# Moving the sums and low parts of shared operands, v's weight sums and the key/value low parts from a choice of two engines to VectorE alone

## The chip, the core and the metric

The kernel runs on one core of one Trainium2 chip. A core has five engines with an instruction queue each: TensorE (PE) multiplies matrices into PSUM, VectorE (DVE) and GpSimd (POOL) do elementwise work, ScalarE (ACT) copies and applies functions, SyncE (SP) here issues the DMAs. Each engine works through its queue in order, and semaphores hold an instruction until its inputs are there. The metric is the device time of one execution in microseconds (us).

## The reference, cut to what matters

One decoder block over 1024 tokens of width 1024, all in float32:

```python
h = x
h = h + hybrid_mixer(rmsnorm(h, norm_mix), w_in, ...)            # Mamba-2 branch and gated linear attention branch
h = h + mem_cross_attention(rmsnorm(h, norm_xattn), rmsnorm(mem, norm_mem), w_xq, w_xkv, w_xo)
h = h + swiglu(rmsnorm(h, norm_ffn), w_ffn_in, w_ffn_out)        # width 2816
return rmsnorm(h, norm_final)
```

`hybrid_mixer` begins with one wide product, `n @ w_in`, whose columns are split into z, xBC, dt, q, k, v, r, a1 and two gates. The cross-attention's keys and values are `m @ w_xkv` of 256 memory tokens. Nearly all the arithmetic is in such products.

## The kernel before

**Products in parts.** TensorE takes float32 operands rounded to a shorter form (`F32R`). To keep float32 accuracy each operand x is split into a high part, `hi = round(x)`, and a low part, `lo = x - hi`, and a product is the sum of three: hi·hi, hi·lo, lo·hi. The helper `split` (line 223) does it: ScalarE writes `hi`, and a subtraction writes `lo`, on the engine given by its argument `e`, or on VectorE if none is given.

**Seven products for eight.** A big product is a two-by-two block product done with seven multiplications (B11, B21, T1, B22, T2, T3, T4; a Strassen-Winograd scheme). For that, sums and differences of blocks are formed on both sides. The side that is shared by many units (the normalised activations) is prepared once by the class `Operands` (lines 231 to 274): for each of the seven names and each k it may first combine two blocks in place (`comb`, line 272; in T1, T2, T3 and T4) and then split the block (line 273) into tiles such as `B11h` and `B11l`. For x the blocks are in tiles `hs`, for the feed-forward part in tiles `o`. `upto` hands the steps out one by one between products. The side of one unit (a stripe of 256 weight columns) is prepared in `Unit.left` (line 295), with sums in tiles `sa` and `raw`.

**The first stages.** `kv_unit` (line 550) computes keys and values of the memory tokens from `w_xkv`: it splits the weights, two blocks of 128 rows at a time, into `whi` and `wlo` (line 563). `x_steps` (line 586) works out the norm of x (`xr`, spread over the partitions by way of `diag` tiles and TensorE) and transposes x into `hs`. `v_steps` (line 637) computes v with the scheme in which the weights are the moving side: it loads the weights into `vraw`, forms their sums in `vsa` and in place (lines 652 to 662), and splits them. A loop at line 699 and the call at line 710 interleave these three. After them come the other column groups of `w_in` with the two recurrences between them (up to about 900 us), five dense products, the attention, and from about 1340 us the feed-forward part, whose shared operands are built while the dense product before it runs (line 1471).

**Who does what.** `either` (line 85) picks VectorE or GpSimd for one instruction while the program is written. It keeps a ledger for each engine (class `Meter`): a guess when the engine will be done, set forward by each instruction that it gets, and by TensorE's own estimated time. GpSimd is taken if it would end earlier by this ledger, with `slack` us in its favour:

```python
def either(ap, slack=0.0):
    return POOL if POOL.after(ap) - slack < DVE.after(ap) else DVE
```

`either` is used at other places too (`Unit.left`, statistics, gates of the feed-forward part). The order of the instructions in each engine's queue is written by the tile framework: it plans all instructions by priority against a simulated clock (`schedule_with_timeline_sim=True`, line 1675); work inside `with ahead():` is given a priority 200 steps earlier. The lines that the program names for elementwise work on both engines are all line 73, the ledger's wrapper; so groups are told apart by their tiles.

Of the kernel before, what the change touches and what calls it, by code (L numbers as in the profile page):

```python
# [78 lines left out]
def block_kernel(ctx: ExitStack, tc: tile.TileContext, t: dict, out: bass.AP):  # L79
# [3 lines left out]
    DVE, POOL = Meter(nc.vector, now, 0.06, 1.04e-3), Meter(nc.gpsimd, now, 0.08, 2.25e-3)  # L83

    def either(ap, slack=0.0):

        return POOL if POOL.after(ap) - slack < DVE.after(ap) else DVE
# [34 lines left out]
    def acc():  # L122
        return ps.tile([P, 512], F32, name="acc", tag="acc", bufs=4)
# [4 lines left out]
    add = lambda e, o, a, b: e.tensor_tensor(o, a, b, ALU.add)  # L128
    sub = lambda e, o, a, b: e.tensor_tensor(o, a, b, ALU.subtract)
# [12 lines left out]
    def slot(key, shape=(P, 2, TOK), dt=F32, name="sl"):  # L142
        pl, n = slots[key]
        return pl.tile(list(shape), dt, name=name, tag="sl", bufs=n)
# [78 lines left out]
    def split(src, hi, lo, e=None):  # L223
        ACT.activation(hi, src, AF.Copy)  # L224
        sub(e or DVE, lo, src, hi)

    def wring():

        return [wp.tile([P, 640], F32R, name=n, tag=n, bufs=3)[:, :528] for n in ("whi", "wlo")]

    class Operands:
# [30 lines left out]
        def build(s, hb, kh, first):  # L262
            blk = hb if callable(hb) else lambda: hb
            for name in s.order:
                new, of, comb = s.PLAN[name]
                o = s.B[name] = [slot(s.last_key if name == "T4" else s.key, (P, kh, HALF), F32R, name=name + x) for x in "hl"]
                for k in range(kh):
                    q = lambda ij: blk()[ij[0] * kh + k][:, half(ij[1] ^ s.swap)]
                    for ij in new:
                        first(ij[0] * kh + k, ij[1] ^ s.swap, q(ij))  # L270
                    if comb:
                        comb[0](either(q(of), 1.0), q(of), q(comb[1]), q(comb[2]))
                    split(q(of), o[0][:, k], o[1][:, k], either(q(of)))
                    yield

    class Unit:
# [37 lines left out]
        def q(s, i, j):  # L314
            return s.o[:, i, half(j)]
# [195 lines left out]
    def load_kv_w(c0):  # L511
        kv_raw[c0] = slot("op", (P, NB, 256), name="raw")
        SP.dma_start(kv_raw[c0], t["w_xkv"][:, c0:c0 + 256].rearrange("(k p) c -> p k c", p=P))
# [36 lines left out]
    def kv_unit(c0):  # L550

        n = kv_cols.index(c0)
        for c in kv_cols[n:n + 4]:
            if c not in kv_raw:
                load_kv_w(c)
        raw = kv_raw[c0]
        pa = [kv_bank[0](), kv_bank[0]()]
        for kk in range(4):
            with ahead():
                hi, lo = wring()  # L560
                hv = hi[:, :512].rearrange("p (k c) -> p k c", c=256)
                lv = lo[:, :512].rearrange("p (k c) -> p k c", c=256)
                split(raw[:, 2 * kk:2 * kk + 2, :], hv, lv, either(lo))
            for i in range(2):
                o = pa[i][:, :256]
                for k2 in range(2):
                    k = 2 * kk + k2
                    for m, (x, y) in enumerate(((hv, mh), (lv, mh), (hv, ml))):
                        w_, m_ = x[:, k2, :], y[:, k, :]
                        if c0 < D:  # L570
                            PE.matmul(o, w_[:, i * P:(i + 1) * P], m_, start=k == 0 and m == 0, stop=k == 7 and m == 2)
                        else:
                            PE.matmul(o, m_[:, i * P:(i + 1) * P], w_, start=k == 0 and m == 0, stop=k == 7 and m == 2)
            yield
        s = stg.tile([P, 2, 256], F32, name="kvs", tag="st")
        for i in range(2):
            if c0 < D:
                mul(DVE, s[:, i], pa[i][:, :256], mbc)
            else:
                ACT.activation(s[:, i], pa[i][:, :256], AF.Copy, scale=mss[:, i:i + 1])  # L580
        if c0 < D:
            SP.dma_start(kT_d[c0:c0 + 256, :].rearrange("(i p) m -> p i m", p=P), s)
        else:
            SP.dma_start(vm_d[:, c0 - D:c0 - D + 256].rearrange("(i p) c -> p i c", p=P), s)
# [40 lines left out]
    def load_v(pr):  # L625
        if pr not in vraw:
            rr = vraw[pr] = [vp.tile([P, 4, 2 * HW], F32, name="vraw", tag=f"vraw{h}") for h in range(2)]
            for i in range(2):
                v0 = V0 + 512 * pr + 256 * i
                a0 = (DT0, A0)[pr] + 8 * i  # L630
                for h in range(2):
                    for c0, n, o in ((v0, 256, i * HW), (a0, 8, i * HW + 256)):
                        SP.dma_start(rr[h][:, :, o:o + n],
                                     w_in[512 * h:512 * h + 512, c0:c0 + n].rearrange("(k p) c -> p k c", p=P))
        return vraw[pr]

    def v_steps():
        for pr in range(2):
            rr = load_v(pr)
            A11, A21 = rr[0][:, :, :HW], rr[0][:, :, HW:]  # L640
            A12, A22 = rr[1][:, :, :HW], rr[1][:, :, HW:]
            s = {ij: vp.tile([P, 4, HW], F32, name="vq", tag=f"vq{ij[0]}{ij[1]}") for ij in
                 ((0, 0), (0, 1), (1, 0), (1, 1))}
            small = (dt_t, a1_t)[pr]

            def vfin(i, j, ap):
                SP.dma_start(v_d[half(j), 512 * pr + 256 * i:512 * pr + 256 * i + 256]
                             .rearrange("(a p) c -> p a c", p=P), ap[:, :, :256])
                POOL.tensor_copy(small[:, 4 * j:4 * j + 4, 8 * i:8 * i + 8], ap[:, :, 256:])

            sa = vp.tile([P, 4, HW], F32, name="vsa", tag="vsa")
            for n, name in enumerate(CHAIN):
                parts = []
                with ahead():
                    e = either(A11, 2.0)
                    if name == "T1":
                        add(e, sa, A21, A22)
                    elif name == "B22":
                        sub(e, sa, sa, A11)
                        sub(either(A11, 2.0), A12, A12, sa)  # L660
                    elif name == "T3":
                        sub(e, A21, A11, A21)
                    a = (A11, A12, sa, A12, sa, A21, A22)[n]
                    for k2 in range(2):
                        hi, lo = wring()
                        hv, lv = hi.rearrange("p (k c) -> p k c", c=HW), lo.rearrange("p (k c) -> p k c", c=HW)
                        split(a[:, 2 * k2:2 * k2 + 2, :], hv, lv)
                        parts.append((hv, lv))
                xh, xl = B[name]
                if n in (0, 2, 4):  # L670
                    pa = [acc()[:, :HW] for _ in range(4)]
                for a4 in range(4):
                    p = pa[a4]
                    m = 0
                    for k in range(4):
                        wh, wl = (q[:, k % 2, :] for q in parts[k // 2])
                        for x, w in ((xh, wh), (xl, wh), (xh, wl)):
                            PE.matmul(p, x[:, k, a4 * P:(a4 + 1) * P], w, start=n in (0, 2, 4) and m == 0, stop=m == 11,
                                      skip_group_check=True)
                            m += 1  # L680
                    g = lambda i, j: s[i, j][:, a4, :]
                    with ahead():
                        if n == 0:
                            ACT.activation(g(1, 0), p, AF.Copy)
                        elif n == 1:
                            ACT.activation(g(0, 0), p, AF.Copy)
                        else:
                            ij = ((1, 1), (0, 1), (0, 1), (1, 1), (1, 0))[n - 2]
                            add(DVE, g(*ij), p, g(*ij) if n > 3 else g(1, 0))
                    B.upto((n + 1) * B.kh + a4 + 1)  # L690
                    yield
                ij = (None, (0, 0), None, None, (0, 1), (1, 1), (1, 0))[n]
                if ij:
                    vfin(*ij, s[ij])

    kvg = chain(kv_unit(c) for c in kv_cols)
    xg = x_steps()
    load_v(0)
# [7 lines left out]
    drain(xg)  # L706
    turn_rest()
    vg = v_steps()
    kv_bank[0] = bank
    run(vg, (kvg, 1.2))  # L710
# [968 lines left out]
```

## Time and profile before

| | |
|---|---|
| median of 3 runs | 1998.22 us (1995.6 to 1999.11) |
| span of the profiled execution | 2000.0 us |
| PE busy | 1933.5 us (97%), 9772 products |
| DVE busy | 1330.8 us (67%), 1869 instructions |
| ACT busy | 866.3 us (43%), 1486 instructions |
| POOL busy | 658.0 us (33%), 482 instructions |
| mean granted TensorE clock | 0.992 |

Everything in the profile is of one execution. A row of a group gives line, engine, operation, `out<-in` by the program's names, shapes and count, then after the bar the busy time and the mean duration in ns, then the idle time of that engine before these instructions and who ended it. A row of a timeline begins with start and length in us; the bracket gives the idle time before it and its releaser. A row of the table by stretch gives start and end, length, and the busy time with the count of PE, PEld (weight loads), DVE, ACT and POOL, then the granted clock, the DMA engines' share and GB/s. A row of waits gives who waited for whom, the total, the number of waits and the longest. Durations of neighbouring instructions overlap by some hundredths of a us, since the end of one runs into the start of the next.

### The profile page before, as it was taken

What the parts mean: (1) busy time and instruction counts of PE and PEld (TensorE: products, weight loads), DVE (VectorE), ACT (ScalarE), POOL (GpSimd) and SP (SyncE); (2) the same over time, 40 slices, a digit from 0 to 9 for tenths busy, and PEclk for the clock granted to TensorE, in tenths of its full rate; (3) what the DMA queues carried; (4) which work ended last, traced back from release to release, by engine and by line L of the source; (5) the groups of instructions that cost most, each with busy time, mean ns of one, the idle gap of its engine ahead of it and who ended that gap; (6) DMA issues with size and microseconds to landing.
All of it is one profiled execution on the core that took longest, in us unless ns stands there. A gap on an engine that the chain in (4) does not pass through costs nothing.

```text
span 2000.0 us, 26313 instructions
## 1 busy us (share of the span) xinstructions
PE 1933.5 (97%) x9772; PEld 1619.0 (81%) x9772; DVE 1330.8 (67%) x1869; ACT 866.3 (43%) x1486; POOL 658.0 (33%) x482
## 2 busy tenths in 40 slices
PE   6899999999999999999999999999999999999998
PEld 6799677787777877888888888877888888878887
DVE  5856579979887566643553427478777777784465
ACT  7434745455553555543223226453333333354243
POOL 3521253445654121112442100155444444430002
PEclk9899999999999999999999999999999999999999
DMA  9332233365663754697674310333224223176463
GB/s 303 137 123 76 97 127 116 107 199 162 181 192 103 213 162 158 226 394 242 252 249 163 106 43 22 126 124 124 79 90 134 93 85 119 72 269 220 153 228 126
DMA packets 242019, 309.59 MB, mean 155 GB/s; under 512 B 16586, under 2 KB 164276, under 8 KB 241892
## 3 DMA queue, kind: packets, MB, share of 16 engines
q1 hardware_dynamic: 241892, 307.92, 46.1%
q8 instruction: 77, 1.26, 0.3%
q14 instruction: 50, 0.41, 0.1%
HBM read 211.07 MB, written 96.80 MB: 154 GB/s over the span
## 4 chain that ended last, share of the span: by engine, by line
PE 69%; DVE 12%; DMA 7%; ACT 5%; issue 3%; POOL 3%; SPq 0%; POOLq 0%; DVEq 0%; ACTq 0%
PE acc L51 61%; PE bank L51 7%; DVE wlo L73 3%; DVE cv L73 2%; DVE o L73 1%; PE bank L55 1%; DMA raw<-in_w_in_dram 1%; DMA h_d<-ga 1%; DMA sr<-sr_d 1%; ACT whi L224 1%; DMA csb<-cs_d 1%; POOL sa L73 1%; DMA xt<-in_x_dram 1%; DMA fr<-act_d 1%; DVE fs L73 1%
## 5 line engine op out<-in xcount | busy, mean ns | idle before, releaser
L51 PE MATMUL acc<-hl,wd 128*128 128x512 f32 x1920 | 439.2, 390 | 0.2 <-DVE hl L73 0.2
L51 PEld LDWEIGHTS acc<-hl,wd 128*128 128x128 f32 x1920 | 360.0, 188 | 75.3 <-DVE hl L73 0.6
L73 DVE TENSOR_TENSOR wlo<-raw,whi 128x512 fp32r<-128x512 f32 x264 | 243.1, 925 | 64.9 <-ACT whi L224 64.5
L224 ACT ACTIVATE whi<-raw 128x512 fp32r<-128x512 f32 x272 | 169.7, 628 | 237.0 <-PE acc L51 208.1
L73 DVE TENSOR_TENSOR o<-acc,o 128x512 f32<-128x512 f32 (+1 forms) x256 | 172.5, 675 | 105.8 <-PE acc L51 91.1
L51 PE MATMUL acc<-fs 128*128 128x512 f32 (+1 forms) x792 | 156.0, 356 | 1.8 <-ACT o L1574 1.7
L51 PEld LDWEIGHTS acc<-fs 128*128 128x128 f32 x792 | 130.6, 189 | 22.8 <-ACT o L1574 2.1
L73 POOL TENSOR_TENSOR raw<-raw,sa 128x512 f32<-128x512 f32 x48 | 65.0, 1354 | 253.8 <-DVE wlo L73 250.8
L224 ACT ACTIVATE fs<-fr 128x1024 fp32r<-128x1024 f32 (+1 forms) x84 | 80.1, 984 | 112.9 <-PE acc L51 38.6
L73 DVE TENSOR_TENSOR fs<-fr,fs 128x1024 fp32r<-128x1024 f32 (+1 forms) x84 | 99.8, 1218 | 38.5 <-ACT fs L224 38.0
L224 ACT ACTIVATE whi<-sa 128x512 fp32r<-128x512 f32 x96 | 59.9, 627 | 107.5 <-PE acc L51 107.4
L73 POOL TENSOR_TENSOR sa<-raw 128x512 f32<-128x512 f32 x47 | 75.8, 1613 | 82.0 <-DMA raw<-in_w_in_dram 44.8
L73 DVE TENSOR_TENSOR wlo<-sa,whi 128x512 fp32r<-128x512 f32 x96 | 82.8, 863 | 19.0 <-ACT whi L224 17.6
L224 ACT ACTIVATE wd<-raw 128x1024 fp32r<-128x1024 f32 x40 | 42.2, 1058 | 104.9 <-PE acc L51 104.4
L73 DVE TENSOR_TENSOR wd<-raw,wd 128x1024 fp32r<-128x1024 f32 x40 | 53.9, 1349 | 50.5 <-ACT wd L224 50.0
L73 POOL TENSOR_TENSOR raw<-raw 128x512 f32<-128x512 f32 x48 | 83.0, 1730 | 5.0 <-DVE sa L73 5.0
L51 PE MATMUL acc<-B21h,whi 128*128 128x512 f32 x192 | 76.3, 398 | 3.1 <-ACT o L353 3.1
L51 PE MATMUL acc<-T1h,whi 128*128 128x512 f32 x192 | 76.3, 397 | 2.8 <-ACT whi L224 2.8
L51 PE MATMUL acc<-B22h,wlo 128*128 128x512 f32 x192 | 77.0, 401 | 1.2 <-DVE wlo L73 1.2
L51 PE MATMUL acc<-B22h,whi 128*128 128x512 f32 x192 | 75.2, 392 | 2.6 <-DVE o L73 1.5
L51 PE MATMUL acc<-T4h,whi 128*128 128x512 f32 x192 | 75.9, 395 | 1.5 <-DVE o L73 1.5
L51 PE MATMUL acc<-T1h,wlo 128*128 128x512 f32 x192 | 76.8, 400 | 0.5 <-DVE wlo L73 0.5
(386 smaller groups left out, 4771.6 us busy)
## 6 DMA issues: line engine op xcount, KB each, us to landing
raw<-in_w_in_dram SPq DMA_DIRECT2D x26, 1024.0 KB, 6.1
raw<-in_w_ffn_in_dram SPq DMA_DIRECT2D x22, 1024.0 KB, 6.3
act_d<-o SPq DMA_DIRECT2D x77, 256.0 KB, 2.1
fr<-act_d SPq DMA_DIRECT2D x35, 512.0 KB, 6.4
pre<-in_w_ffn_out_dram SPq DMA_DIRECT2D x11, 1024.0 KB, 6.1
fr<-down_d SPq DMA_DIRECT2D x20, 512.0 KB, 3.7
down_d<-pre SPq DMA_DIRECT2D x33, 256.0 KB, 5.2
raw<-in_w_xkv_dram SPq DMA_DIRECT2D x8, 1024.0 KB
```

The costliest lines, as they stand in the source:

```text
L51: return s.e.matmul(o, x, y, **kw)
L55: return s.e.transpose(o, x, i)
L73: return f(*a, **kw)
L224: ACT.activation(hi, src, AF.Copy)
```

## The change

At three places the choice between VectorE and GpSimd is taken away and VectorE is named. In `Operands.build` these are the combinations of blocks and the low parts; in `kv_unit` the low parts of the key/value weights; in `v_steps` the sums of v's weights. `split` without its last argument uses VectorE. Nothing else in the program text changes; the ledgers that `either` reads elsewhere are still kept.

```diff
@@ Operands.build
                     if comb:
-                        comb[0](either(q(of), 1.0), q(of), q(comb[1]), q(comb[2]))
-                    split(q(of), o[0][:, k], o[1][:, k], either(q(of)))
+                        comb[0](DVE, q(of), q(comb[1]), q(comb[2]))
+                    split(q(of), o[0][:, k], o[1][:, k])
@@ kv_unit
-                split(raw[:, 2 * kk:2 * kk + 2, :], hv, lv, either(lo))
+                split(raw[:, 2 * kk:2 * kk + 2, :], hv, lv)
@@ v_steps
-                    e = either(A11, 2.0)
                     if name == "T1":
-                        add(e, sa, A21, A22)
+                        add(DVE, sa, A21, A22)
                     elif name == "B22":
-                        sub(e, sa, sa, A11)
-                        sub(either(A11, 2.0), A12, A12, sa)
+                        sub(DVE, sa, sa, A11)
+                        sub(DVE, A12, A12, sa)
                     elif name == "T3":
-                        sub(e, A21, A11, A21)
+                        sub(DVE, A21, A11, A21)
```

## The prediction

> **What bounds the kernel now.** I read the page's engine totals and its chain first.
>
> ```profile
> PE 1933.5 (97%) x9772; PEld 1619.0 (81%) x9772; DVE 1330.8 (67%) x1869; ACT 866.3 (43%) x1486; POOL 658.0 (33%) x482
> PE 69%; DVE 12%; DMA 7%; ACT 5%; issue 3%; POOL 3%; SPq 0%; POOLq 0%; DVEq 0%; ACTq 0%
> ```
>
> TensorE (PE) is busy for 97% of the span, so a change on VectorE (DVE) and GpSimd (POOL) can only matter where PE stands still. The edits touch three places: the preparation of x, mem and v (up to about 180 us) and the operands of the feed-forward part (about 1260 to 1360 us). So the next view is the table of busy time by stretch. Its columns are the stretch, its length, then busy time and count of PE, PEld, DVE, ACT and POOL, the granted clock, and the DMA share and rate.
>
> ```profile
> 22.20:44.60 22.40, 16.35 (x125) 14.98 (x123) 15.14 (x20) 15.28 (x32) 13.82 (x11) 0.91 0.82 249
> 44.60:73.90 29.30, 19.18 (x126) 17.91 (x125) 29.28 (x28) 16.67 (x34) 22.71 (x14) 0.78 0.70 253
> 73.90:118.80 44.90, 44.74 (x368) 44.47 (x369) 32.85 (x52) 19.97 (x37) 7.37 (x5) 1.00 0.15 51
> 130.00:200.00 70.00, 70.00 (x488) 65.69 (x487) 38.14 (x71) 29.68 (x54) 16.29 (x21) 1.00 0.30 96
> 1336.00:1362.00 26.00, 22.10 (x93) 17.38 (x92) 26.00 (x27) 15.02 (x28) 19.15 (x13) 0.93 0.38 127
> ```
>
> In 44.6 to 73.9 us (call it B) DVE works without a pause, 29.28 of 29.30 us, while PE is idle for 10 us and its clock drops to 0.78. The same holds for 1336 to 1362 us (C): DVE 26.00 of 26.00, PE idle 3.9 us. Between them PE is full (44.74 of 44.90, 70.00 of 70.00). The view of waits says what PE waits for:
>
> ```profile
> PE bank L51 <- DVE wlo L73: 6.4, 1, 6.4
> PE bank L51 <- DVE diag L73: 5.0, 2, 4.3
> PE acc L51 <- ACT o L353: 2.3, 1, 2.3
> ```
>
> The first two lie before 75 us, the third in C, where that ACT copy stands behind DVE work. In all three places the bound is DVE's queue, and the change puts more work on it. The question is whether this work costs DVE more or less than what GpSimd's running beside it costs now.
>
> **What moves.** The groups of GpSimd that the three edits name:
>
> ```profile
> L73 POOL TENSOR_TENSOR hs<-hs 128x512 f32<-128x512 f32 x14 | 22.7, 1648 | 7.6 <-DVE B11l L73 6.4 <-DVE T1l L73 1.3
> L73 POOL TENSOR_TENSOR wlo<-raw,whi 128x512 fp32r<-128x512 f32 x8 | 10.7, 1352 | 20.7 <-ACT whi L224 18.5 <-PE bank L55 2.2
> L73 POOL TENSOR_TENSOR vsa<-vraw 128x1056 f32<-128x1056 f32 x2 | 5.4, 2702 | 8.5 <-DMA vraw<-in_w_in_dram 8.5
> L73 POOL TENSOR_TENSOR vraw<-vraw 128x1056 f32<-128x1056 f32 x2 | 5.2, 2600 | 0.1
> L73 POOL TENSOR_TENSOR vsa<-vsa,vraw 128x1056 f32<-128x1056 f32 x2 | 4.9, 2470 | 4.5 <-DVE wlo L73 4.5
> L73 POOL TENSOR_TENSOR B11l<-o,B11h 128x512 fp32r<-128x512 f32 x4 | 5.4, 1343 | 160.1 <-ACT B11h L224 160.1
> L73 POOL TENSOR_TENSOR B22l<-o,B22h 128x512 fp32r<-128x512 f32 x2 | 3.5, 1750 | 0.0
> L73 POOL TENSOR_TENSOR B21l<-o,B21h 128x512 fp32r<-128x512 f32 x1 | 1.3, 1291 | 3.5 <-ACT B21h L224 3.5
> L73 POOL TENSOR_TENSOR o<-o x12: 1285/1396/1799, 1273.7 to 1349.3; 128x512 f32<-128x512 f32 x12
> ```
>
> That is 47 instructions: 14 combinations of x's blocks, 8 low parts of key/value weights, 6 sums of v's weights, and in the feed-forward part 7 low parts and 12 combinations. The low parts of x's operands are on DVE already. No DMA and no TensorE work moves.
>
> What does one cost on DVE? Look at a moment when GpSimd rests, and at an operation that reads only one operand from SBUF (the other comes from PSUM):
>
> ```profile
> 75.76 1.89 DVE L73 TENSOR_TENSOR B22l<-hs,B22h 128x512 fp32r<-128x512 f32 x3
> 75.00:80.00 5.00, 5.00 (x44) 5.00 (x43) 3.67 (x7) 2.25 (x6) 0.00 (x0) 1.00 0.20 67
> L73 DVE SCALAR_TENSOR_TENSOR hs<-bank,cols,rbc 128x512 f32<-128x512 f32 x8 | 5.7, 742 | 1.8 <-ACT rbc L598 1.8
> L73 DVE TENSOR_TENSOR B21l<-hs,B21h 128x512 fp32r<-128x512 f32 x4 | 6.2, 1586 | 0.0
> L73 DVE COPY cols<-bank 128x90 f32<-128x90 f32 x1 | 0.2, 240 | 0.0
> ```
>
> With GpSimd silent, three 128x512 operations take 1.89 us, 0.63 us each. The same shape takes 1586 ns (B21l) in B, where GpSimd is busy 22.71 us; the last three rows are DVE's groups in B. The eight operations from PSUM take 742 ns in that same stretch. So it isn't a slow DVE: operations with two SBUF operands, and only these, are held while GpSimd runs. GpSimd's share of the work is paid for on DVE.
>
> **A, 22.2 to 44.6 us.**
>
> ```profile
> 22.32 1.28 POOL L73 TENSOR_TENSOR wlo<-raw,whi 128x512 fp32r<-128x512 f32 x1 [14.08 <-ACT whi L224]
> 24.76 0.48 DVE L73 TENSOR_SCALAR diag<-ident,xr 128x128 f32<-128x128 f32 x2 [1.13 <-POOL xr L73]
> 27.22 1.11 DVE L73 TENSOR_SCALAR diag<-ident,xr 128x128 f32<-128x128 f32 x1 [1.25 <-PE bank L51]
> 33.46 1.50 DVE L73 TENSOR_SCALAR diag<-ident,xr 128x128 f32<-128x128 f32 x2
> 37.48 2.84 DVE L73 TENSOR_TENSOR wlo<-vraw,whi 128x528 fp32r<-128x528 f32 x1
> 40.24 2.62 DVE L73 TENSOR_SCALAR diag<-ident,xr 128x128 f32<-128x128 f32 x2
> 37.32 2.44 POOL L73 TENSOR_TENSOR vsa<-vraw 128x1056 f32<-128x1056 f32 x1 [2.64 <-DMA vraw<-in_w_in_dram]
> 39.83 2.75 POOL L73 TENSOR_TENSOR vraw<-vraw 128x1056 f32<-128x1056 f32 x1
> L73 DVE TENSOR_TENSOR vraw<-vraw,vsa 128x1056 f32<-128x1056 f32 x2 | 2.5, 1252 | 2.6 <-POOL vsa L73 2.6
> ```
>
> Time freed on the chain: the first low part, 1.28 to 0.63, 0.65; the diag at 27.22, 1.11 against 0.24 (half of the pair of 0.48), 0.87; the pair at 33.46, 1.50 against 0.48, 1.02; the wlo at 37.48, 2.84 against about 0.65 (528 columns), 2.19; the pair at 40.24, which ends as the 1056-column operation does, 2.62 against 0.48, 2.14. Sum 6.9. Added to DVE: five low parts at 0.63 and two sums of v's weights at 1.25, 5.65. All of it on the path leaves 1.2; all hidden in DVE's 7.3 idle us (22.40 less 15.14) leaves 6.9. I take 3, nearer the lower end, since the two sums can't start before their load lands at 37.3 and the last idle gap before 44.6 is short. Queued behind them are the diag pair, PE's 4.3 us wait, and everything of B.
>
> **B, 44.6 to 73.9 us.** Of its 28 DVE instructions eight come from PSUM and one is the small copy; the other 19 have two SBUF operands. Unheld: 19 x 0.63 + 8 x 0.70 + 0.24 = 17.8 us. The four combinations of T1 must come before the T1 low parts: 4 x 0.63, 20.3. The ten others (T2 to T4) may fall here, 6.3 more, 26.6, or later. So the stretch shortens by 2.7 to 9.0 us. I take 6, about half of the ten inside. PE, busy 19.18 us at a lowered clock, isn't the floor.
>
> What carries the gain on: behind 73.9 PE is full. There the left-over combinations, three low parts and one 1.25 us sum lie on DVE's 12 idle us (44.90 less 32.85), at price 0; if that cover is gone, each costs PE 0.63. The second half of v (sums at 1.25 each) lies under PE's 70.00 of 70.00, DVE 38.14: 0.
>
> **C, 1336 to 1362 us, and before it.**
>
> ```profile
> L73 DVE TENSOR_TENSOR T2l<-o,T2h 128x512 fp32r<-128x512 f32 x4 | 4.8, 1228 | 0.0
> L73 POOL TENSOR_TENSOR o<-o 128x512 f32<-128x512 f32 x3 | 4.9, 1646 | 2.6 <-ACT o L1469 2.6
> L73 POOL TENSOR_TENSOR raw<-raw,sa 128x512 f32<-128x512 f32 x2 | 3.5, 1751 | 3.0 <-DVE rstd L73 3.0
> L73 POOL TENSOR_TENSOR raw<-raw 128x512 f32<-128x512 f32 x2 | 3.0, 1512 | 0.0
> L73 POOL TENSOR_TENSOR sa<-raw 128x512 f32<-128x512 f32 x2 | 2.8, 1390 | 1.2 <-DVE wlo L73 1.2
> 1310.00:1320.00 10.00, 10.00 (x46) 8.29 (x45) 5.67 (x7) 3.96 (x6) 4.34 (x5) 1.00 0.30 107
> ```
>
> Up to 1336 PE is full and DVE half idle (1310 to 1320: 5.67 of 10), so the 14 instructions moved there cost nothing. In C, 22 of the 27 DVE instructions have two SBUF operands, at a mean near 1.23 us. Unheld they take 13.9, the five others some 1.9, and the five moved in (two B22l, three combinations) 3.15: 19 of 26 us, 7 gained. But the six sums of the first weight units stay on GpSimd; a DVE operation caught behind one ends 1.1 us later (1751 less 630), 6.6 for six, which leaves 0.4. Above, PE caps it: 3.9 idle and 7% of 22.1 in clock, 5.4. I take 2.5.
>
> **A choice that shifts.** `either` weighs DVE's ledger against GpSimd's at other places too, and it will now see a fuller DVE. A few statistics sums near C may go to GpSimd; each holds DVE by up to 1.1, inside C's range. The planner's re-ordering I can't price from rows; it is a rival.
>
> **Sum.** 3 + 6 + 2.5 = 11.5 us; ends 1.2 + 2.7 + 0.4 = 4.3 and 6.9 + 9.0 + 5.4 = 21.3. The profiled execution's span is 2000.0 us, 1.8 above the runs' median of 1998.2, so the rows stand for the runs. 1998.2 less 11.5 is 1986.7: 1987, one's own range 1977 to 1994.
>
> **One term a page would change.**
>
> ```profile
> 65.00:70.00 5.00, 3.49 (x16) 3.49 (x17) 5.00 (x4) 0.64 (x1) 4.37 (x4) 0.50 0.00 0
> ```
>
> Behind PE's 6.4 us wait the clock is 0.50 for 3.49 busy us. I give a restored clock nothing, since B ends on DVE. The Trainium skill, "TensorE: Matmul & The Clock Gate" (Part 1), has the clock fall to half after an idle window of about 3.4 us. By it a wait cut below that keeps the full clock; if PE's work then counted, 1.7 us (half of 3.49) would come on top, 1985.
>
> **Rivals.**
> 1. The other side: the long DVE times are not GpSimd's doing and stay. Then the moved work is simply added to a full queue: 14 x 0.63 in B (8.8), 5.65 in A, 3.15 in C: 17.6 slower, 2016. It decides once the hold per operation falls by less than 17.6 over the some 46 held ones (19, 5 and 22), 0.38 us; B's mean hold is (29.28 - 17.8) / 19 = 0.60. The 0.63 at 75.76 and the even 742 ns speak against it; that B22l has other data at another time leaves a little. Chance 0.10. The Trainium skill, "Perfetto Trace Analysis" (Optimizing Scalar/DVE Operations), says that work of a saturated VectorE may be worth giving to GpSimd, which would speak for this rival, but adds that the two share an SBUF read port, so it might not help; the rows side with the second half.
> 2. A poor order inside the stretches: T2 to T4 stand before what PE waits for, nothing of A is hidden. The lower ends: 1994. Chance 0.18.
> 3. Hidden anyway: the gain of A and B is given back before 130 us, because the left-over combinations make PE wait for low parts in 73.9 to 118.8: 14 waits of 0.63 are 8.8 of the 9; with C's lower end, about 1998. DVE's 12 idle us there speak against it. Chance 0.10.
> 4. The queues are planned anew from a simulated clock, and a stretch without any edit gets a worse order. By the size of A and B together it could take 9 and more with C at nothing: 1999 to 2006, say 2003. Chance 0.10.
>
> **Chances.** The forecast has 0.52. Faster by over 0.2% (4 us, about what a measurement of this kernel tells from no change): forecast and rival 2, 0.70. Within: rival 3, 0.10. Slower: rivals 1 and 4, 0.20. The range, 1978 to 2004, leaves out rival 1 and the tails of the forecast and rival 4.
>
> **What would show it.** Right: no GpSimd group hs, wlo, vsa or B..l; B21l and T1l near 0.65 us in the first 75 us; the diag pairs near 0.5; PE's waits of 6.4 and 4.3 shortened; PE's full stretch starting some 9 us earlier; T2l to T4l shorter near 1340. Wrong: DVE operations of 1.2 us and more without GpSimd beside them; DVE waiting for a load with diag or hs behind it; new PE waits between 75 and 130 us.

## The result and the profile after

The changed kernel takes 1994.14 us (median of 20 runs, 1990.88 to 1998.51) against 1998.16 us for the kernel before on the same chip (20 runs): a ratio of 0.9976, 95% interval 0.9968 to 0.9984. A second measurement of the same change gave 0.9973 (0.9964 to 0.9982), 5.4 us. So the change gains 4 to 5.4 us where 11.5 were forecast: the right direction, less than half of the size.

The totals by engine on the page of the changed kernel:

```profile
PE 1933.7 (97%) x9772; PEld 1619.8 (81%) x9772; DVE 1328.6 (67%) x1908; ACT 866.3 (44%) x1486; POOL 603.0 (30%) x443
```

GpSimd has 39 instructions fewer and VectorE 39 more, though 47 were named by the edits: `either` gave eight others (on tiles `o`) to GpSimd. VectorE's busy time is 2.2 us lower with 39 more instructions, which is the first sign that the price of the moved work was right.

One profile is one execution, and the first one of before turned out to be a long one (span 2000.0; a run's time is some 1.7 us over its span). I took two more of each kernel and cut all six at the same events: ScalarE's first pass over x (`hs<-xt`, which the expectations call the first copy of x), the first `B11l`, the first product with `T1l`, the first T1 product of the next column group, and the last T1 product of the feed-forward part. A and B are thus longer than the stretches of the prediction with these names (22.2 to 44.6 and 44.6 to 73.9 us), and lie around them.

| stretch, us | before, three profiles | after, three profiles | mean change | forecast |
|---|---|---|---|---|
| start to the first pass over x (no edit lies there) | 16.7, 15.7, 17.0 | 15.7, 15.8, 15.6 | -0.8 | 0 |
| A: to the first B11l | 31.2, 28.5, 29.5 | 30.3, 29.2, 29.6 | 0.0 | -3 |
| B: to the first T1 product | 38.3, 38.3, 38.3 | 33.0, 35.1, 34.5 | -4.1 | -6 |
| v: to the next column group's first T1 product | 92.9, 93.1, 92.8 | 91.8, 92.2, 91.8 | -1.0 | 0 |
| to the last T1 product, C inside | 1577.8, 1575.7, 1576.6 | 1575.3, 1575.1, 1575.3 | -1.5 | -2.5 |
| the rest | 243.1, 243.6, 243.3 | 243.1, 242.4, 243.0 | -0.5 | 0 |
| span | 2000.0, 1994.9, 1997.5 | 1989.2, 1989.8, 1989.8 | -7.9 | -11.5 |

The spans of these six differ by more than the medians of many runs do (7.9 against 4.0 and 5.4), so the table says where the time went, and the ratios say how much. What it says of A is that nothing was gained; of B, that two thirds of the forecast came; of the rest, that nothing was given back behind B.

A, B and v by stretch, first of the kernel before, then of the changed one, with the columns of the prediction's table:

```profile
16.70:47.90 31.20, 24.74 (x182) 22.71 (x181) 19.99 (x29) 23.74 (x47) 13.82 (x11) 0.89 0.89 287
47.90:86.20 38.30, 28.59 (x214) 27.98 (x215) 34.61 (x38) 22.24 (x46) 23.24 (x15) 0.87 0.54 193
86.20:179.10 92.90, 90.79 (x725) 88.86 (x724) 56.57 (x95) 30.01 (x54) 23.31 (x18) 1.00 0.27 86
```

```profile
15.70:46.00 30.30, 25.76 (x186) 23.33 (x185) 19.74 (x36) 23.43 (x47) 4.04 (x4) 0.90 0.92 298
46.00:79.00 33.00, 28.09 (x219) 26.59 (x219) 30.05 (x52) 22.87 (x47) 2.14 (x1) 0.99 0.67 232
79.00:170.80 91.80, 90.00 (x724) 88.61 (x723) 59.88 (x101) 30.14 (x54) 9.08 (x11) 1.00 0.28 87
```

In B VectorE does 52 instructions in 30.05 us where it did 38 in 34.61. PE's 28 us of products are the same (28.59 and 28.09); its idle time falls from 9.7 to 4.9 us and its clock rises from 0.87 to 0.99. The groups of VectorE in B of the changed kernel:

```profile
L73 DVE TENSOR_TENSOR hs<-hs 128x512 f32<-128x512 f32 x16 | 10.4, 682 | 0.0
...
L73 DVE TENSOR_TENSOR B21l<-hs,B21h 128x512 fp32r<-128x512 f32 x4 | 2.6, 679 | 0.0
```

The 1586 ns of `B21l` have become 679, without an edit to that line. All 16 combinations of x's blocks are in this stretch. What PE now waits for, up to 90 us, in the view of waits:

```profile
PE bank L55 <- ACT xs L608: 4.2, 4, 3.5
PE bank L51 <- DVE wlo L73: 3.5, 3, 1.9
```

The 6.4 and 4.3 us are gone. In their place stand 1.9 for a low part, and a new wait of 3.5 for ScalarE.

**Why A gained nothing.** VectorE and then ScalarE of the changed kernel, on the timeline:

```profile
36.72 1.26 DVE L73 TENSOR_TENSOR vsa<-vraw 128x1056 f32<-128x1056 f32 x1 [0.84 <-DMA vraw<-in_w_in_dram]
...
39.22 0.47 DVE L73 TENSOR_SCALAR diag<-ident,xr 128x128 f32<-128x128 f32 x2
...
39.53 0.63 ACT L224 ACTIVATE whi<-raw 128x512 fp32r<-128x512 f32 x1 [3.02 <-DMA raw<-in_w_xkv_dram]
```

The diag pair takes 0.47 us, as forecast. Ahead of it VectorE waits 0.84 us for the load of v's weights and then does the sum, 1.26: 2.1 us which lay on GpSimd before, where nobody queued behind them. But these 2.1 us aren't what PE waits for. The chain of work that ended last (start, length, what) runs elsewhere:

```profile
32.16 7.29 DMA raw<-in_w_xkv_dram
...
39.53 0.63 ACT whi L224
40.16 0.50 ACT xs L608
...
40.70 1.11 PE bank L55 x4
41.81 0.87 PE bank L51 x4
...
42.70 0.61 ACT rbc L598
```

ScalarE, an engine that the change doesn't touch, now has the rounding of the next key/value weights (39.53) ahead of two copies of x, and waits 3.02 us for that load. The copies empty the PSUM banks for PE's next transposes of x (PE's wait of 3.5), and the diag product comes behind these, at 41.6; VectorE had the diag pair ready at 39.7. The chain has the same steps in all three profiles of the changed kernel, and in that of `first_only` below. ScalarE before had it the other way round, with the copies done by 38.6 and the rounding behind the spread norm:

```profile
43.98 0.60 ACT L598 ACTIVATE rbc<-bank 128x512 f32<-128x512 f32 x1 [5.41 <-PE bank L51]
44.48 0.62 ACT L224 ACTIVATE whi<-raw 128x512 fp32r<-128x512 f32 x1
```

And what was to be gained was smaller than the first profile showed. In the second profile of before, VectorE and GpSimd:

```profile
37.14 0.47 DVE L73 TENSOR_SCALAR diag<-ident,xr 128x128 f32<-128x128 f32 x2
38.11 2.43 POOL L73 TENSOR_TENSOR vsa<-vraw 128x1056 f32<-128x1056 f32 x1 [4.39 <-DMA vraw<-in_w_in_dram]
```

Here the load landed when VectorE was already past its diag pair, so this sum held nothing; the one behind it held a low part of the key/value weights instead (2.11 us at 41.49). In the third profile the pair was held for 2.62 us again. The holds of 2.2 and 2.1 us which the prediction counted in A depend on which comes first in one execution. With `ffn_only` below, which has A as before, A takes 27.8 to 31.2 us in four executions of before; in four with all of A's edits (`first_only` has them too) it takes 29.2 to 30.3.

**Why B gained less.** VectorE of the changed kernel from 62 us on, and PE's wait at its end:

```profile
62.02 1.89 DVE L73 TENSOR_TENSOR hs<-hs 128x512 f32<-128x512 f32 x3
...
64.44 2.49 DVE L73 TENSOR_TENSOR hs<-hs 128x512 f32<-128x512 f32 x4
...
68.07 2.49 DVE L73 TENSOR_TENSOR B22l<-hs,B22h 128x512 fp32r<-128x512 f32 x4
...
71.08 1.89 DVE L73 TENSOR_TENSOR wlo<-raw,whi 128x512 fp32r<-128x512 f32 x3
71.82 0.39 PE L51 MATMUL bank<-mh,wlo 128*128 128x256 f32 x1 [1.87 <-DVE wlo L73]
```

The combinations of T2 to T4, which PE doesn't need before 79, stand ahead of the low parts that it needs at 70. None of them was left over.

**C.** Kernel before, then the changed one, each cut from the last dense product on (0 to 13 us, 13 to 26, 60 to 100):

```profile
1338.70:1351.70 13.00, 10.72 (x45) 8.81 (x44) 13.00 (x12) 9.46 (x18) 9.70 (x6) 0.87 0.31 98
1351.70:1364.70 13.00, 11.38 (x54) 8.67 (x53) 13.00 (x17) 3.50 (x6) 8.86 (x6) 1.00 0.38 126
...
1398.70:1438.70 40.00, 40.00 (x179) 33.11 (x178) 29.30 (x38) 13.72 (x24) 18.43 (x13) 1.00 0.30 101
```

```profile
1329.00:1342.00 13.00, 11.72 (x50) 9.58 (x49) 13.00 (x22) 9.64 (x19) 2.08 (x2) 0.87 0.48 156
1342.00:1355.00 13.00, 12.37 (x61) 10.43 (x60) 10.84 (x17) 4.09 (x7) 11.88 (x7) 1.00 0.21 68
...
1389.00:1429.00 40.00, 38.87 (x170) 31.76 (x170) 32.94 (x40) 12.91 (x23) 19.34 (x13) 1.00 0.39 128
```

In the first 26 us PE works 2.0 us more (24.09 against 22.10), close to the 2.5 of the forecast. The low parts there, 1228 ns each before, have the price of B:

```profile
L73 DVE TENSOR_TENSOR T2l<-o,T2h 128x512 fp32r<-128x512 f32 x4 | 2.6, 679 | 0.0
```

Thirty us later PE loses 1.1 us where before it was full (38.87 of 40). The timeline there:

```profile
1367.62 5.91 POOL L73 TENSOR_TENSOR o<-o,ssum 128x512 f32<-128x512 f32 x4 [4.57 <-DVE o L73]
...
1385.80 1.78 DVE L73 TENSOR_TENSOR o<-o 128x512 f32<-128x512 f32 x1
...
1391.61 0.63 ACT L1430 ACTIVATE o<-o 128x512 f32<-128x512 f32 x1 [4.61 <-DVE o L73]
...
1392.81 0.50 PE L51 MATMUL acc<-B11h,whi 128*128 128x512 f32 x1 [0.92 <-ACT whi L224]
```

GpSimd now does eleven operations on tiles `o` of the gates and products in a row from 1367.6 to 1383.6, where it had five in the kernel before; this choice is `either`'s, which sees a fuller ledger of VectorE (the kernel with the feed-forward edit alone has the same eleven). The unit's sums of weights come behind them, and these hold VectorE (1.78 us for an operation of 0.68). VectorE is late for ScalarE's gate (the wait of 4.61), and the weights behind the gate in ScalarE's queue are late for PE.

### The profile page after: what moved, and what is told of

The parts are those of the page before. It is cut to its first block, busy times and chain, and to the rows that moved or that the text cites. A ratio compares the mean times of both kernels' runs of the same rounds, so it can differ in the third digit from the quotient of the medians.

```text
span 1989.2 us, 26282 instructions
## 1 busy us (share of the span) xinstructions
PE 1933.7 (97%) x9772; PEld 1619.8 (81%) x9772; DVE 1328.6 (67%) x1908; ACT 866.3 (44%) x1486; POOL 603.0 (30%) x443
## 3 DMA queue, kind: packets, MB, share of 16 engines
q8 instruction: 77, 1.26, 0.3%
## 4 chain that ended last, share of the span: by engine, by line
PE 70%; DVE 10%; DMA 5%; ACT 5%; issue 4%; POOL 3%; SPq 1%; POOLq 0%; ACTq 0%; DVEq 0%
PE acc L51 61%; PE bank L51 8%; DVE wlo L73 2%; DVE o L73 2%; DVE cv L73 2%; PE bank L55 1%; DMA sr<-sr_d 1%; DMA xt<-in_x_dram 1%; DMA csb<-cs_d 1%; ACT whi L224 1%; DMA bd<-bd_d 1%; POOL sa L73 1%; DVE fs L73 1%; DMA fr<-act_d 1%; POOL o L73 1%
## 5 line engine op out<-in xcount | busy, mean ns | idle before, releaser
L73 POOL TENSOR_TENSOR raw<-raw,sa 128x512 f32<-128x512 f32 x48 | 69.2, 1443 | 256.9 <-DVE wlo L73 246.0
L224 ACT ACTIVATE fs<-fr 128x1024 fp32r<-128x1024 f32 (+1 forms) x84 | 80.1, 984 | 112.8 <-PE acc L51 40.5
L73 DVE TENSOR_TENSOR fs<-fr,fs 128x1024 fp32r<-128x1024 f32 (+1 forms) x84 | 99.8, 1219 | 39.7 <-ACT fs L224 39.2
L51 PE MATMUL acc<-B11h,whi 128*128 128x512 f32 x192 | 75.8, 395 | 3.2 <-ACT whi L224 3.2
```

The lines of the kernel that those rows point to most:

```text
L51: return s.e.matmul(o, x, y, **kw)
L73: return f(*a, **kw)
```

## The experiments

The ratio is always against the kernel before on the same chip, with its 95% interval. All short diffs are against the kernel before, if nothing else is said. A and B are those of the table, in the run's one profile.

**The two kernels again.** Nothing edited.

> The changed kernel once more, for a second profile. In the first pair of profiles everything from the first T1 product of v on runs 8.2 us earlier, the end 10.8 us, while the medians of 20 runs differ by 4.0. Theory 1 (the gain is fixed, the first profile of before was a long execution): the first T1 product of v starts at 79 us again, and the median lies 4 to 5 us under that of before. Theory 2 (the early gain is there in some executions only): the first T1 product starts 2 us or more later than 79.0 in this profile.

> The kernel before once more, for a second profile. Theory 1: it shows the first T1 product of v earlier than the 86.2 us of the first profile, near 83, since the medians differ by 4 and not by 8; a stretch of the first 75 us is then the one that varies. Theory 3 (the early 8 us are fixed, and some 4 us are given back later): 86.2 again, and a later stretch shorter than in the first profile.

> A further profile of the kernel before. If the first profile's hold of 2.84 and 2.62 us on VectorE in the first stretch was the rarer course of that kernel, the stretch from ScalarE's first copy of x to the first B11l is again 28 to 29 us; if it is the usual course, 31 us.

> A further profile of the changed kernel. The stretch from ScalarE's first copy of x to the first B11l is 29 to 30.5 us and the next one, to the first T1 product, 33 to 36.6 us, depending on whether a PE wait of over 2 us near 72 us is followed by a half clock.

Measured: the changed kernel again 1991.56 us, 0.9973 (0.9964 to 0.9982); the kernel before under the same conditions 1998.78, 1.0006 (0.9997 to 1.0015). The profiles are the second and third numbers in the cells of the table. The runs of the third profiles took 1999.24 and 1991.51 us. The first T1 product of v stands at 80.1 us in the second profile of the changed kernel (79.0 in the first) and at 82.5 in that of before (86.2), nearer to Theory 1 than to the others. (The 8.2 us in the first expectation is nearly the distance at the next column group, 8.3; at the first T1 product of v it is 7.2.) The hold of the diag pair came in two of three executions of before, and A of the third fell between the guesses (29.5). B of the kernel before is 38.3 in all three; B of the changed one varies by 2.1.

**One edit at a time.** The edit of x's operands alone, with the low parts and combinations of the feed-forward part left to `either`:

```diff
-  comb[0](either(q(of), 1.0), q(of), ...)
+  comb[0](DVE if s.order == tuple(s.PLAN) else either(q(of), 1.0), q(of), ...)
-  split(..., either(q(of)))
+  split(..., None if s.order == tuple(s.PLAN) else either(q(of)))
```

> Only x's operands are on VectorE; key/value low parts, v's sums and the feed-forward operands keep the choice. From the first B11l to the first T1 product before takes 38.3, 38.3 and 38.5 us in three profiles, the changed kernel 33.0, 35.1 and (without the feed-forward edit) 36.6. The forecast's theory on the hold: this stretch falls by 3 us or more here too, the time by 2 to 4 us. Rival (the order of the queue eats it, since eight combinations stand ahead of the v low parts that TensorE waits for): less than 1 us.

Measured: 1996.43 us, 0.9996 (0.9987 to 1.0005); A 28.8, B 40.0. The time is the rival's, under 1 us; B grew by 1.7 us where the theory had it fall by 3. But this isn't the edit of x's operands alone: `either`, with a fuller ledger of VectorE, gave nine other low parts of the key/value weights to GpSimd, 17 where the kernel before has 8 and has none from 35 to 92 us. The holds have changed sides. VectorE and GpSimd of this kernel:

```profile
60.73 4.90 DVE L73 TENSOR_TENSOR hs<-hs 128x512 f32<-128x512 f32 x8
65.54 1.89 DVE L73 TENSOR_TENSOR B22l<-hs,B22h 128x512 fp32r<-128x512 f32 x3
65.69 4.71 POOL L73 TENSOR_TENSOR wlo<-raw,whi 128x512 fp32r<-128x512 f32 x1 [23.55 <-DVE hs L73]
73.75 1.28 POOL L73 TENSOR_TENSOR wlo<-raw,whi 128x512 fp32r<-128x512 f32 x1 [3.36 <-ACT whi L224]
```

VectorE's operations follow each other without a gap until 69.28, and one low part that `either` moved to GpSimd takes 4.71 us instead of 1.28: it ends at 70.40, 1.1 us behind the last of them. In the view of waits PE stands 4.3 us for that low part.

The key/value low parts alone:

```diff
-  split(raw[:, 2 * kk:2 * kk + 2, :], hv, lv, either(lo))
+  split(raw[:, 2 * kk:2 * kk + 2, :], hv, lv)
```

> Only the low parts of the key/value weights are made by VectorE. If holds by GpSimd count operation by operation, eight fewer GpSimd operations of 1.35 us should free about 8 x 0.6 = 4.8 us of VectorE's queue for 8 x 0.65 = 5.2 us added, so about no change, within 2 us of the kernel before. If what PE waits for (the low parts of B) is what decides, a low part made without being starved by back-to-back VectorE combinations comes earlier and the kernel gains 1 to 3 us. If the edits only work together, the kernel is up to 2 us slower.

Measured: 1998.03 us, 0.9997 (0.9987 to 1.0007); A 28.7, B 39.4. The first of the expectations, no change, came. VectorE and GpSimd:

```profile
58.74 5.71 DVE L73 TENSOR_TENSOR T1l<-hs,T1h 128x512 fp32r<-128x512 f32 x4
64.38 3.42 DVE L73 TENSOR_TENSOR wlo<-raw,whi 128x512 fp32r<-128x512 f32 x2
60.58 10.08 POOL L73 TENSOR_TENSOR hs<-hs 128x512 f32<-128x512 f32 x6 [0.63 <-DVE T1l L73]
```

Now GpSimd's combinations hold VectorE's low parts, 1.7 us each instead of 0.68, and PE waits twice for 4.4 us for such low parts.

The sums of v's weights alone:

```diff
-  add(e, sa, A21, A22)
+  add(DVE, sa, A21, A22)
   # the three other sums of v likewise
```

> Only v's sums are on VectorE, everything else as before. Theory 4: the first B11l no earlier than 44 us in any execution, vsa waiting for its load in VectorE's queue ahead of the diag pair, the time 0 to 3 us slower than before. The forecast's theory on A: 2 us faster, since the diag pair isn't held any more.

Measured: 2003.62 us, 1.0029 (1.0017 to 1.0040), slower by 5.8 us, more than either theory had; A 27.9, B 39.7. In A the load had landed in time, so the sum stood ahead of the diag pair without a wait. Behind B, in v, the time from the first to the last T1 product is 71.7 us against 65.9 in the first profile of before. The load of v's second half is issued 43.1 us after the first T1 product instead of 39.7, and VectorE waits for it with two low parts and a result behind it (PE's waits in v are 6.5 us against 2.1):

```profile
138.19 1.26 DVE L73 TENSOR_TENSOR vsa<-vraw 128x1056 f32<-128x1056 f32 x1 [2.48 <-DMA vraw<-in_w_in_dram]
```

`either` shifted work here too: five other operations went to GpSimd, three of them low parts of x's operands. So the loss isn't shown to be that of the sums alone.

The feed-forward part alone (the first two lines of the first diff with the condition turned round):

> Only the feed-forward operands are on VectorE; x, key/value and v keep the choice. Forecast's theory: 1 us faster than before by the shift seen in the first pair (9.7 before 1336 us, 10.8 behind), 2.5 by the forecast. Rival: 4 us, all of the measured gain.

Measured: 1995.08 us, 0.9995 (0.9986 to 1.0003), and in its profile C reads as in the changed kernel (PE 23.77 of the first 26 us, 38.87 of 40 later). That is some 1 us, which the interval doesn't tell from nothing.

**Edits together.** x, key/value and v on VectorE, the feed-forward part by `either`; then x and key/value alone:

> All edits in x's operands, the key/value low parts and v's sums; the feed-forward operands keep the choice between the engines. Forecast's theory (A and B give 9, C gives 2.5 of 11.5): three quarters of the whole gain, about 3 of the 4 us measured. Rival (the gain of A and B is given back, C carries the rest): within 1 us of before.

Measured: 1992.69 us, 0.9980 (0.9971 to 0.9988), 4.0 us of the changed kernel's gain, as the forecast's theory has it; A 30.1, B 36.6.

> Low parts of the key/value weights and the operands of x on VectorE, v's sums and the feed-forward part by the choice of two engines. If v's sums on VectorE cost the changed kernel 2 us in the first stretch and the feed-forward edit brings 1 us, this is about 1 us slower than the version that leaves only v's sums on GpSimd: 1991 us, 6 us under the kernel before. If the v edit costs nothing, it equals the kernel with x, kv and v on VectorE: 1992.7. If the choice of two engines takes VectorE for v's sums anyway, the same 1992.7 to 1993.

Measured: 1993.56 us, 0.9976 (0.9965 to 0.9986); B 34.7. Its profile is of the longest of its 12 runs, so only B is read from it. Two edits whose 0.8 and 0.6 us alone can't be told from nothing bring 4.8 together. By the times this is at the edge of the noise (3.4 us more than the sum of the two, with some 3.4 of noise by the three intervals); by B it is clear, 1.7 and 1.1 us longer alone and 3.6 shorter together. In `kv_only` the combinations left on GpSimd hold the low parts, in `x_only` the low parts that `either` moved there are held; the gain comes when GpSimd has fallen silent in B. v's sums, which stay on GpSimd here, add nothing that shows (0.9976 without them on VectorE, 0.9980 with).

**The hold itself.** The changed kernel, and GpSimd gets one addition for each of 16 low parts of x's operands, which reads the high part and writes a tile that nobody reads (the tile's own line isn't shown):

```diff
   split(q(of), o[0][:, k], o[1][:, k])
+  if s.order == tuple(s.PLAN) and name in ("B11", "B21", "T1", "B22"):
+      h = o[0][:, k].bitcast(F32)
+      nc.gpsimd.tensor_tensor(dummy, h, h, ALU.add)
```

> The changed kernel with 16 more GpSimd additions of 128x512, each reading a finished high part (of B11, B21, T1, B22 of x) and writing a tile that nobody reads; VectorE's own work and order stay. Theory on the hold: VectorE's B11l, B21l, hs and T1l take 1.0 us and more on average again instead of 0.68, the stretch from the first B11l to the first T1 product grows by 5 to 10 us, and the median is 4 to 9 us above the changed kernel's, at or over before's. Rival (rival 1 of the forecast: the long durations are not GpSimd's doing): durations stay at 0.68 and the time at the changed kernel's.

Measured: 1999.23 us, 1.0007 (0.9999 to 1.0016), so the whole gain is gone; B is 40.7 us. Groups of VectorE from 44 to 90 us:

```profile
L73 DVE SCALAR_TENSOR_TENSOR hs<-bank,cols,rbc 128x512 f32<-128x512 f32 x8 | 5.7, 741 | 1.3 <-ACT rbc L602 1.3
L73 DVE TENSOR_TENSOR B11l<-hs,B11h 128x512 fp32r<-128x512 f32 x4 | 4.8, 1226 | 0.0
L73 DVE TENSOR_TENSOR B21l<-hs,B21h 128x512 fp32r<-128x512 f32 x4 | 4.4, 1146 | 0.0
L73 DVE TENSOR_TENSOR T1l<-hs,T1h 128x512 fp32r<-128x512 f32 x4 | 2.6, 678 | 0.0
```

And of the last four additions in the view of their tile (shortest, median and longest in ns, first and last start):

```profile
L277 POOL TENSOR_TENSOR dummy<-B22h x4: 1042/1368/10964, 70.6 to 84.2; 128x512 f32<-128x512 f32 x4
```

VectorE's work is that of the changed kernel, 52 instructions in B. Where an addition of GpSimd runs beside it (`B11l`, `B21l`), it takes 1.1 to 1.2 us; where none does (`T1l`, behind the third group of additions, so not at the 1.0 us of the expectation), 678 ns; the operations from PSUM stay at 741. So GpSimd's running beside VectorE is what the long durations were; its reads and its writes weren't tried apart.

**Without A's new wait.** The changed kernel, with three of v's four sums on GpSimd:

```diff
@@ against the changed kernel
-  add(DVE, sa, A21, A22)
+  add(POOL, sa, A21, A22)
-  sub(DVE, sa, sa, A11)
+  sub(POOL, sa, sa, A11)
-  sub(DVE, A21, A11, A21)
+  sub(POOL, A21, A11, A21)
```

> The changed kernel with three of the four sums of v's weights put back on GpSimd (all but the difference that was on VectorE before too). In the two profiles of the changed kernel the sum vsa stands in VectorE's queue ahead of two hs and the diag pair and waits for its load there, and the first B11l starts at 46.0 and 45.0 us; in the usual executions of before it starts at 44.2 and 43.5. Theory 4 (this wait in the queue eats what A and B gain): the first B11l at 42 to 44, the first T1 product 2 to 3 us earlier than in the changed kernel's 79 to 80, the median 1 to 3 us under the changed kernel's. Rival (the hold alone counts, so GpSimd's sums cost more than they free): as the changed kernel or 1 to 3 us slower.

Measured: 1990.22 us (5 runs), 0.9965 (0.9952 to 0.9977); A 29.0, B 33.1. It is the fastest kernel of all here, ahead of the changed one in the median; the intervals of the two ratios overlap, so the some 2 us between them are likely, not settled. GpSimd and VectorE:

```profile
34.61 3.38 DVE L73 SCALAR_TENSOR_TENSOR hs<-bank,cols,rbc 128x512 f32<-128x512 f32 x5
37.39 2.44 POOL L73 TENSOR_TENSOR vsa<-vraw 128x1056 f32<-128x1056 f32 x1 [5.62 <-DMA vraw<-in_w_in_dram]
37.91 2.21 DVE L73 TENSOR_SCALAR diag<-ident,xr 128x128 f32<-128x128 f32 x2
```

GpSimd waits 5.62 us for the load and nobody minds; VectorE does its five operations on x at once. In this execution the sum then held the diag pair (2.21), and A is still no longer than in the changed kernel. Its chain too begins with the load of the key/value weights, at 33.2 us, and goes by ScalarE's rounding to a low part that GpSimd's second sum holds for 2.15 us. So VectorE's wait for v's weights wasn't what kept A long. The time is the one of Theory 4, but its signs didn't come (the first `B11l` at 45.5 us, the first T1 product at 78.6); where the 2 us come from isn't shown.

## Why the prediction was wrong, step by step

**The price of the work: right.** It said that an operation with two SBUF operands costs 0.63 us on VectorE, and that its length of 1.2 us and more was GpSimd's doing. Measured: 0.68 for all of them in B (0.62 from start to start, 2.49 us for four), VectorE 2.2 us less busy with 39 more instructions, and the long durations back with the added reads. Rival 1 (2016 us) falls with that. The Trainium skill, "SBUF — State Buffer" (Who interferes with whom), says that an operation of VectorE with two SBUF inputs and a GpSimd operation that reads SBUF exclude each other, and that the one which starts first keeps the other waiting to its end; the rows of the added additions agree that each is held by the other (1.1 to 1.2 us for VectorE, 10.96 for one GpSimd addition), though 10.96 is far more than one operation's wait.

**A, 3 taken, 0 measured: this step failed.** "In all three places the bound is DVE's queue" holds for A in two of three executions of before, and in none of the changed kernel. With the holds gone the limit is the load of the next key/value weights, which lands at 39.0 to 39.5 us in its three profiles, with ScalarE's rounding waiting for it ahead of the copies of x: in the first profile VectorE has the diag pair ready at 39.7 and PE takes it up at 41.6. The prediction gave this load no term; it looked at v's load on VectorE alone ("the two sums can't start before their load lands at 37.3"), and listed under what would prove it wrong a wait of VectorE for a load. That wait came, 0.84 us, but isn't on the chain. Also its 4.3 us of holds came from one execution, which was 3.5 us over the median and not 1.8, since 2000.0 is a span; another had none of the two. The order of ScalarE's queue is new as well: the profiles show the rounding ahead of copies of x in the kernels with the key/value low parts on VectorE; in the one with x's operands alone ScalarE spreads the norm (`rbc`) before it rounds, as before. No edit names it; it is the planner's, rival 4 in small. How much of A the order cost, and how much the load would have cost in any order, no run separates.

**B, 6 taken, 4.1 measured: mis-sized.** The step is "about half of the ten inside". All of them were, ahead of the low parts that PE waits for, and the stretch came out near the lower part of its range of 2.7 to 9.0. In `first_only`, with the same edits, B is 36.6, 1.7 us less than before; the clock below has to do with that. That PE isn't the floor was right up to 70 us; behind the wait there PE is full to the end of B (28.09 of 33.00 us busy in all).

**C, 2.5 taken, 2.0 measured, 1.1 given back.** The term was right in its place. That `either` shifts work to GpSimd stood in the prediction, "inside C's range"; the shift came 30 us later, and with it the first PE waits at a place which had none.

**Behind B: right.** Rival 3 (the gain given back before 130 us) falls: from the first T1 product to the next column group the changed kernel is 1.0 us shorter, not longer. That gain wasn't forecast. GpSimd's busy time there fell from 23.31 to 9.08 us; that this is its cause was not tried alone, and v's sums by themselves went the other way.

**What came is rival 2**: a poor order inside the stretches and nothing gained in A, 1994 us, given 0.18. Its number is in part luck: it adds 1.2, 2.7 and 0.4, and the stretches gave 0, 4.1 and 0.9, 5.0 in all against the 4.0 and 5.4 of the medians. The prediction had A's lower end in hand, and B's queue order was open, yet both terms were taken above their lower ends at once.

**The clock.** The prediction gave a restored clock nothing and told of a rule by which it would bring 1.7 us. PE's clock (last but two) in the same two us of two executions of the changed kernel, each behind one wait of PE, of 1.87 us in the first and 1.88 us in the third:

```profile
72.00:74.00 2.00, 2.00 (x18) 2.00 (x19) 0.97 (x2) 0.57 (x1) 1.04 (x1) 1.00 0.60 211
```

```profile
72.00:74.00 2.00, 2.00 (x12) 2.00 (x11) 0.54 (x2) 0.63 (x1) 0.24 (x1) 0.51 0.19 66
```

The same wait halves the clock in one execution and not in the other, and 18 products become 12. That is most of the difference between B of 33.0 and of 34.5. In the second profile the wait is 2.37 us, in `first_only` 2.76. Behind it the products run at half clock for 0 us in the first profile (B 33.0), 3.4 in the third (34.5), 3.5 in the second (35.1) and 6.2 in `first_only` (36.6). PE is full from there to the end of B, so half of the slow time is lost; taken off, it leaves 33 to 33.5 us in all four, an estimate from these numbers. So the clock makes nearly all of the spread of B, and the reason for giving it no term, "since B ends on DVE", failed: in the changed kernel B ends on PE. The Trainium skill, "TensorE: Matmul & The Clock Gate" (Part 1), has the fall after an idle window of about 3.4 us which runs freely; the third execution shows it after 1.88 us, so a wait cut below 3.4 us doesn't keep the full clock for sure.

## What to carry to other kernels

Work on two engines that hold each other up is best moved as a whole: taken from GpSimd in one place only, what is left there holds or is held, and x's operands and the key/value low parts brought 0.8 and 0.6 us alone but 4.8 together. Where a ledger picks the engine, a choice fixed at one place moves others: eight operations here, nine and five in the runs with one edit, so count them by tile before reading a run as one edit. When the queue that bounds a stretch is relieved, look for the next limit on the chain before counting the relief as gain: here it was a load with a rounding waiting for it, on an engine without an edit. A hold that depends on when a load lands is read from several executions, and where the order in a queue is open, the lower end is the better forecast.

## What was not expected of the hardware

VectorE, working without a gap, can hold a GpSimd operation of 1.3 us until it takes 4.71 us, and in the kernel with the added additions one took 10.96 us: holds go both ways, and a GpSimd operation need not come in between two operations of VectorE. In the kernel before the two engines took turns (seven of GpSimd's combinations in 11.36 us, beside low parts of up to 1.77 us); why they do so there and not here no run shows. And a wait of 1.9 us on TensorE halved its clock for some 3 us in one execution and left it at 1.00 in another.
